# Grams of three chunks moved ahead of the inverses, attention's output product by high and low halves, one weight chunk's place changed

## The chip, the cores and the metric

The kernel runs on one core of a Trainium2 chip. The metric is device time in microseconds (us), the median of three runs; lower is better. TensorE (PE in the profile) does the matrix products, VectorE (DVE) and ScalarE (ACT) the work on elements, GpSimd (POOL) a few small things, and SyncE (SP) issues the weight transfers.

## What is computed

One decoder layer on a sequence of 256 tokens of width 2048, in float32: two token mixers side by side (mLSTM and RWKV-7), merged by gates; cross-attention to 256 memory tokens; a causal convolution with GeGLU. What the change touches is the RWKV-7 scan and the attention's output:

```python
def rwkv7_scan(r, w, k, v, kk, kka):
    def step(state, inp):
        rt, wt, kt, vt, kkt, kat = inp
        state = (state * wt[:, :, None, :]
                 - jnp.einsum('bhvk,bhk->bhv', state, kkt)[..., None] * kat[:, :, None, :]
                 + vt[..., None] * kt[:, :, None, :])
        return state, jnp.einsum('bhvk,bhk->bhv', state, rt)
...
    p = jax.nn.softmax(scores, axis=-1).astype(v.dtype)
    o = jnp.einsum('bhsm,bmhd->bshd', p, v).reshape(B, S, XATTN_WIDTH)
    return o @ wo
```

## The kernel before

**Weights.** Nearly all time goes into products of activations with weights that stream from memory in 648 chunks of 128 x 1024 numbers. A float32 chunk is split: ScalarE casts the high half (wh, L391), VectorE subtracts it for the low half (wl, L421), and TensorE forms three products high x high, low x high, high x low in float32r. In the profile "fm" are such products with 256 columns (the weight held, activations moving) and "tm" those with 512 columns. A chunk's buffer comes free when TensorE has done with the chunk four places earlier, so cast and low half of chunk c+3 are queued when chunk c begins. KICK (L342) lists chunks whose halves are placed some elements further on in their buffer; it changes nothing in the arithmetic.

**Side work.** Everything else is written as Python generators, and the order of all instructions is fixed when the program is written. Twice per chunk (`half()`, called a half step here: six 512-column or twelve 256-column products) the class Spread lets side work run. Each half step adds 640 to VectorE's account and 820 to ScalarE's, up to 1200; a piece of queued work is taken when both accounts are above zero, and what it issues through the metered engines is charged (VectorE 70 + 1.04 per element of a partition, ScalarE 200 + 0.83). Work issued through `nc.vector` and `nc.scalar` isn't charged. A task with a chain runs a piece every so many half steps, whenever neither account is below -700.

**RWKV.** The 256 tokens are cut into 4 chunks of 64; 16 heads are held as 8 pairs (j and e, in two groups hf of four pairs). For each chunk the kernel needs the products of BK (keys) with KR (queries) of all heads, the gram, and the inverse of a unit triangular matrix made from its corner, in 32 x 32 blocks. The task `inverses` (L925) forms the corners alone with 64 small products (gramA), in two bursts; it gathers all 32 x 32 blocks side by side in `comp`, transposes them to A, solves all of them at once on VectorE in 31 steps of a product and a sum (tmp and L), and transposes the result twice into cmt: directly from L, and from Lt, a copy that ScalarE makes with two axes exchanged. When the inverses and the values are there, `start_rwkv` adds the task `rwkv` (L1017), a piece every 3 half steps. Its first piece forms the gram of chunk 0, the next one copies the inverse of chunk 0 to m0 (`diagonal`), the third forms the level-one products (lv) with m0. Then each chunk goes through X, level two, U, the new state (Tn) and the output Y, and while chunk c does that, the gram of chunk c+1 is formed in two halves, one between X and level two and one ahead of U. A gram uses PSUM tiles of the tag aux, of which there are four; sums over heads (bon) use the same tag. U (7) and T2 (6) are tags of larger buffers that all stages share.

**Attention.** The values (xv) come from a tm block whose two halves of columns end one after the other, the probabilities (pT) from four staggered softmax tasks. `xo` (L1719) multiplies them in float32, 8 products, each shown as two records of the profile, and splits the result into oT's halves for the next weight block.

Of the kernel before, what the change touches and what calls it, by code (L numbers as in the profile page):

```python
# [145 lines left out]
def _layer(ctx, tc, nc, d, dbg):  # L146
# [189 lines left out]
    def block(kind, srcs, xs, evac, before=None, cols=512, pool_=None, pre=None, bankwise=False, tail=0):  # L336
# [6 lines left out]
            168: 0, 216: 2, 219: 2, 236: 2, 243: 2, 257: 2, 282: 2}  # L343
# [581 lines left out]
    def inverses():  # L925
# [8 lines left out]
        comp = C("comp", "bg0", [P, 32, 32])  # L934
        for hc in range(4):
            hf, c0 = hc // 2, hc % 2 * 2
            if hc % 2 == 0:
                qs = [aux("gramA", [P, 2, 4, 64]) for _ in range(2)]
                for c in range(4):
                    for j in range(4):  # L940
                        for e in range(2):
                            p = hf * 4 + j
                            mm(qs[c // 2][E2[e], c % 2, j], KR[E2[e], p, c, 0], BK[E2[e], p, c, e])
            q = qs[hc % 2]
            o = comp[:, :, hc * 8:hc * 8 + 8].rearrange("p s u -> p u s")
            v = q.rearrange("p a j s -> p (a j) s")
            dve.tensor_scalar(o, v[:, :, 0:32], ccol("bd", 1), None, op0=ALU.mult)
            dve.scalar_tensor_tensor(o, v[:, :, 32:64], ccol("bd", 1, 32), o, op0=ALU.mult, op1=ALU.add)
            yield
        A = C("A", "au1", [P, 32, 32])  # L950
# [3 lines left out]
        for j in range(31):  # L954

            n = j + 1, 31 - j
# [6 lines left out]
        M["cmt"] = U("cmt", [P, 2, 32, 32])  # L963
        dve.transpose(flat(M["cmt"][:, 0]), flat(L))
        Lt = C("Lt", "au1", [P, 32, 32])
# [51 lines left out]
    def rwkv():  # L1017
# [6 lines left out]
        bg = [C("bg", f"bg{hf}", [P, 2, 512]) for hf in H]  # L1024
        bkt = [bg[hf][:, 0].rearrange("p (j t) -> p j t", j=4) for hf in H]
        gx = [C("gx", f"gx{hf}", [P, 512]) for hf in H]
        gr = [[v.rearrange("p (e j t) -> p e j t", e=2, j=4) for v in (bg[hf][:, 1], gx[hf])] for hf in H]
        au = [C("au", f"au{hf}", [P, 2, 2, 4, 64]) for hf in H]
        ab, uv = [v[:, 0] for v in au], [v[:, 1] for v in au]
# [5 lines left out]
        def gram(c, hf):  # L1035
# [5 lines left out]
            def evac():  # L1041
                for e in H:
                    dve.tensor_mul(ab[hf][:, e], qs[e][:, :, 0:64], bc(sm, 4))
                    dve.tensor_mul(gr[hf][c % 2][:, e], qs[e][:, :, 64:128], bc(im, 4))
            return evac

# [4 lines left out]
        def inverse(c, hf, k):  # L1051
            return cmt[:, k, :, hf * 16 + c * 4:hf * 16 + c * 4 + 4].rearrange("p s j -> p j s")
# [16 lines left out]
        def carried(c):  # L1069
            for hf in H:  # L1070
                for e in H:
                    act.copy(ab[hf][E2[e], e], KR[E2[e], hf * 4:hf * 4 + 4, c, 0])
# [8 lines left out]
        def level1(q, v, more):  # L1081
            for hf, j, e in heads:
                mm(v[quart[1][e], hf, j], ab[hf][quart[0][e], e, j, 32:64], m0[quart[0][e], hf, j])
# [8 lines left out]
        evs = [gram(0, hf) for hf in H]  # L1092
        for ev in evs:
            ev()
        yield
# [4 lines left out]
        level1(*quarter("lv1", 0, (0, 1), True), True)()  # L1100
# [941 lines left out]
```

## Time and profile before

| | |
|---|---|
| median of 3 runs | 1867.37 us (1866.93 to 1867.52) |
| the profiled execution's own time | 1867.02 us |
| its span, first to last instruction | 1865.2 us |
| TensorE busy | 1856.8 us, 15022 products and as many weight loads |
| VectorE busy | 1294.6 us |
| ScalarE busy | 1015.9 us |
| mean granted TensorE clock | 0.999 |

The profile is one execution, taken by the hardware profiler. A product's record covers more than the time until the next one may start, so records overlap: what a product costs TensorE is read from the distance between two starts. Times in a timeline count from the first instruction; merged rows carry xN. "idle before" is time in which an engine had nothing to do, and the name behind it is what it waited for.

### The profile page before, as it was taken

The numbers are of one execution on the slowest core, as the hardware profiler recorded it, in microseconds if no ns is written. First come the engines' busy times: TensorE is split into PE (matmuls) and PEld (weight loads), VectorE is DVE, ScalarE is ACT, GpSimd is POOL, SyncE is SP. The second block draws the span as 40 slices with busy tenths as digits, with TensorE's granted clock in tenths as the row PEclk, the third lists the DMA queues.
The fourth block names the chain that finished last, engine by engine and source line by source line (L and its number), as shares of the span: only waits on it lengthen the run. The fifth ranks groups of instructions, "written<-read, shape, count | busy, mean of one in ns | idle before, by whom it ended". The sixth has DMA issues, their size and how long they took to land.

```text
span 1865.2 us, 36357 instructions
## 1 busy us (share of the span) xinstructions
PE 1856.8 (100%) x15022; PEld 1770.4 (95%) x15022; DVE 1294.6 (69%) x1836; ACT 1015.9 (54%) x1481; POOL 19.9 (1%) x38
## 2 busy tenths in 40 slices
PE   9999999999999999999999999999999999999998
PEld 9999888999999999999999999999999988888887
DVE  7789787666675857687766667776666775556555
ACT  6776445655454646665544445544444554545544
POOL 0000000000000000000000000000000000000000
PEclk9999999999999999999999999999999999999999
DMA  7545544344555765455666666666666666666664
GB/s 264 190 169 195 180 157 159 127 157 159 169 194 196 280 196 180 160 184 173 197 193 196 194 193 195 188 194 197 197 194 194 196 192 214 197 192 192 194 192 145
DMA packets 98197, 351.46 MB, mean 188 GB/s; under 512 B 11056, under 2 KB 11568, under 8 KB 97648
## 3 DMA queue, kind: packets, MB, share of 16 engines
q1 hardware_dynamic: 97168, 348.01, 58.1%
q8 instruction: 117, 1.92, 0.4%
q10 hardware_dynamic: 864, 1.15, 0.2%
q14 instruction: 48, 0.39, 0.1%
HBM read 347.01 MB, written 2.10 MB: 187 GB/s over the span
## 4 chain that ended last, share of the span: by engine, by line
PE 98%; DVE 1%; issue 0%; DMA 0%; ACT 0%; ACTq 0%; DVEq 0%
PE fm L181 68%; PE tm L181 25%; PE gram L181 0%; DVE wl L421 0%; PE Y L181 0%; PE num L181 0%; DMA w<-in_w_in_dram 0%; PE lv L181 0%; DVE ql L66 0%; PE X L181 0%; PE U L181 0%; PE gramA L181 0%; PE zg L181 0%; DVE z L66 0%; PE zwa L181 0%
## 5 line engine op out<-in xcount | busy, mean ns | idle before, releaser
L421 DVE TENSOR_TENSOR wl<-raw,wh 128x1024 fp32r<-128x1024 f32 (+1 forms) x639 | 774.9, 1218 | 412.3 <-ACT wh L391 407.5
L391 ACT CAST wh<-raw 128x1024 fp32r<-128x1024 f32 (+1 forms) x639 | 663.5, 1043 | 481.7 <-PE fm L181 362.3
L181 PE MATMUL fm<-fh,wh 128*128 128x256 f32 x2048 | 564.4, 277 | 0.6 <-DVE fh L66 0.6
L181 PE MATMUL fm<-fh,wl 128*128 128x256 f32 x2048 | 563.4, 276 | 0.0
L181 PE MATMUL fm<-fl,wh 128*128 128x256 f32 x2048 | 563.3, 276 | 0.0
L181 PEld LDWEIGHTS fm<-fh,wh 128*128 128x128 f32 x2048 | 383.6, 188 | 0.8 <-DVE fh L66 0.8
L181 PEld LDWEIGHTS fm<-fl,wh 128*128 128x128 f32 x2048 | 383.5, 188 | 0.0
L181 PEld LDWEIGHTS fm<-fh,wl 128*128 128x128 f32 x2048 | 383.4, 188 | 0.0
L181 PE MATMUL tm<-wh,as 128*128 128x512 f32 x1024 | 315.4, 389 | 0.0
L181 PE MATMUL fm<-hh,wh 128*128 128x256 f32 x1024 | 284.1, 279 | 0.4 <-ACT wh L402 0.3
L181 PE MATMUL fm<-hh,wl 128*128 128x256 f32 x1024 | 281.5, 277 | 0.1
L181 PE MATMUL fm<-hl,wh 128*128 128x256 f32 x1024 | 281.3, 277 | 0.0
L181 PEld LDWEIGHTS tm<-wh,as 128*128 128x128 f32 x1024 | 192.1, 188 | 39.9
L181 PE MATMUL tm<-wl,as 128*128 128x512 f32 x512 | 199.2, 389 | 0.0
L181 PEld LDWEIGHTS fm<-hh,wh 128*128 128x128 f32 x1024 | 191.7, 188 | 2.1 <-ACT wh L402 0.5
L181 PEld LDWEIGHTS fm<-hh,wl 128*128 128x128 f32 x1024 | 191.5, 188 | 0.3 <-DVE wl L421 0.3
L181 PEld LDWEIGHTS fm<-hl,wh 128*128 128x128 f32 x1024 | 191.4, 188 | 0.1
L181 PEld LDWEIGHTS tm<-wl,as 128*128 128x128 f32 x512 | 96.1, 188 | 19.9
L66 ACT CAST as<-ac 128x256 fp32r<-128x256 f32 x128 | 45.6, 404 | 110.8 <-PE tm L181 110.8
L66 DVE TENSOR_TENSOR as<-ac,as 128x256 fp32r<-128x256 f32 x128 | 48.5, 421 | 61.7 <-ACT as L66 61.7
L181 PE MATMUL fm<-mgh,wh 128*128 128x256 f32 x256 | 70.9, 277 | 0.0
L181 PE MATMUL fm<-mgl,wh 128*128 128x256 f32 x256 | 70.8, 276 | 0.0
(386 smaller groups left out, 2214.7 us busy)
## 6 DMA issues: line engine op xcount, KB each, us to landing
raw<-in_w_fu_dram SPq DMA_DIRECT2D x256, 512.0 KB, 4.1
raw<-in_w_in_dram SPq DMA_DIRECT2D x152, 512.0 KB, 3.5
raw<-in_w_fd_dram SPq DMA_DIRECT2D x128, 512.0 KB, 4.0
raw<-in_w_br_dram SPq DMA_DIRECT2D x32, 512.0 KB, 3.8
raw<-in_w_mo_dram SPq DMA_DIRECT2D x32, 512.0 KB, 4.0
raw<-in_w_xk_dram SPq DMA_DIRECT2D x8, 512.0 KB, 3.6
raw<-in_w_xv_dram SPq DMA_DIRECT2D x8, 512.0 KB, 3.5
raw<-in_w_xq_dram SPq DMA_DIRECT2D x8, 512.0 KB, 4.0
```

The costliest lines, as they stand in the source:

```text
L66: return f(out, *a, **k)
L181: pe.matmul(out, lhsT, rhs, start=start, stop=stop, skip_group_check=True)
L391: nc.scalar.copy(wh, r)
L421: nc.vector.tensor_sub(wl, r, self.st[self.nl][0])
```

## The change

The grams of chunks 0, 1 and 2 are formed at the start of `inverses`, in three bursts of three pieces each, and `comp` takes its blocks from them by ScalarE copies; only chunk 3's corners are still made by gramA, with operands exchanged. The products' masked results are kept: chunks 0 and 1 in four T2 tiles, chunk 2 partly in a new U tile (gr2), whose other half is L. The block solve runs on the transposed blocks, so the roles of L and Lt for the two halves of cmt are exchanged. In `rwkv` the first piece is gone, only chunk 3's gram is left in the loop, `early` charges VectorE's account for the others, and the task starts 1 half step after the inverses instead of 4. The attention's probabilities and values are kept as float32r halves, and the output product becomes three float32r products instead of one float32 product. One entry of KICK goes from 282 to 284. Cut to its core:

```diff
-            168: 0, 216: 2, 219: 2, 236: 2, 243: 2, 257: 2, 282: 2}
+            168: 0, 216: 2, 219: 2, 236: 2, 243: 2, 257: 2, 284: 2}
...
-        L = C("L", "au0", [P, 32, 32])
+        sm, im = ccol("sm", 64), ccol("im", 64)
+        comp = C("comp", "bg0", [P, 32, 32])
+        at = comp.rearrange("p t u -> p u t")
...
+        M["ab"] = [[T2("ab", [P, 2, 4, 64]) for _ in range(2)] for _ in range(2)] + [late, late]
+        M["cmt"] = U("cmt", [P, 2, 32, 32])
+
+        def gram(c):
+            ab = M["ab"][c]
+            gr = [M["gr"][hf][c % 2] for hf in range(2)]
+            if c == 2:
+                M["gr2"] = U("gr2", [P, 2, 1024])
...
+            qs = [[aux("gram", [P, 4, 128]) for _ in range(2)] for _ in range(2)]
+            for hf in range(2):
+                for j in range(4):
+                    for e in range(2):
+                        mm(qs[hf][e][:, j], flat(BK[E2[e], hf * 4 + j, c]), flat(KR[E2[e], hf * 4 + j, c]))
+            for hf in range(2):
+                for e in range(2):
+                    nc.vector.tensor_mul(ab[hf][:, e], qs[hf][e][:, :, 0:64], bc(sm, 4))
+                    nc.vector.tensor_mul(gr[hf][:, e], qs[hf][e][:, :, 64:128], bc(im, 4))
+                yield
+            for hf in range(2):
+                for e in range(2):
+                    for b in range(2):
+                        r = slice(e * 64 + b * 32, e * 64 + b * 32 + 32)
+                        nc.scalar.copy(at[r, c * 8 + hf * 4:c * 8 + hf * 4 + 4], ab[hf][r, e, :, b * 32:b * 32 + 32])
+            yield
+
+        def paced(gen):
+            for _ in gen:
+                dve.spent += 672.5
+                yield
+
+        yield from paced(gram(0))
+        yield from paced(gram(1))
+        yield from paced(gram(2))
+        L = M["gr2"][:, 1].rearrange("p (c i) -> p c i", c=32)
         pool.memset(L, 0.0)
...
-        for hc in range(4):
-            hf, c0 = hc // 2, hc % 2 * 2
-            if hc % 2 == 0:
-                qs = [aux("gramA", [P, 2, 4, 64]) for _ in range(2)]
-                for c in range(4):
-                    for j in range(4):
-                        for e in range(2):
-                            p = hf * 4 + j
-                            mm(qs[c // 2][E2[e], c % 2, j], KR[E2[e], p, c, 0], BK[E2[e], p, c, e])
...
+        q = aux("gramA", [P, 8, 64])
+        for p in range(8):
+            for e in range(2):
+                mm(q[E2[e], p], BK[E2[e], p, 3, e], KR[E2[e], p, 3, 0])
...
-            dve.tensor_tensor(o, L[:, 0:j + 1, j].unsqueeze(2).broadcast_to((P,) + n),
-                              A[:, j, j + 1:32].unsqueeze(1).broadcast_to((P,) + n), op=ALU.mult)
-            dve.tensor_add(L[:, 0:j + 1, j + 1:32], L[:, 0:j + 1, j + 1:32], o)
+            dve.tensor_tensor(o, A[:, j + 1:32, j].unsqueeze(2).broadcast_to((P,) + n),
+                              L[:, j, 0:j + 1].unsqueeze(1).broadcast_to((P,) + n), op=ALU.mult)
+            dve.tensor_add(L[:, j + 1:32, 0:j + 1], L[:, j + 1:32, 0:j + 1], o)
...
-        dve.transpose(flat(M["cmt"][:, 0]), flat(L))
+        dve.transpose(flat(M["cmt"][:, 1]), flat(L))
...
-        dve.transpose(flat(M["cmt"][:, 1]), flat(Lt))
+        dve.transpose(flat(M["cmt"][:, 0]), flat(Lt))
...
-            tasks["r"] = side.add(rwkv(), chain=GAP, phase=4)
+            tasks["r"] = side.add(rwkv(), chain=GAP, phase=1)
...
+        def early():
+            dve.spent += 1345.0
...
-        evs = [gram(0, hf) for hf in H]
-        for ev in evs:
-            ev()
-        yield
         diagonal(0)
...
-                ev.append(gram(c + 1, 0))
+                ev.append(gram(c + 1, 0) if c == 2 else early)
...
-                ev.append(gram(c + 1, 1))
+                ev.append(gram(c + 1, 1) if c == 2 else early)
...
+            if c == 0:
+                for hf in H:
+                    nc.scalar.copy(gr[hf][0].rearrange("p e j t -> p (e j t)"), M["gr2"][:, 0, hf * 512:hf * 512 + 512])
...
+            nc.vector.scalar_tensor_tensor(M["xvl"][t][:, c], ps[g][:, t], stm.rc[:, t:t + 1], M["xv"][:, t, c],
+                                           op0=ALU.mult, op1=ALU.subtract)
...
         act.copy(M["pT", h], q)
+        nc.vector.tensor_sub(M["pl"][:, h], q, M["pT", h])
...
-                    mm(q[:, j], M["xv"][:, mt, h * P:(h + 1) * P], M["pT", h][:, mt], start=(mt == 0), stop=(mt == 1))
+                    mm(q[:, j], M["xv"][:, mt, c], M["pT", h][:, mt], start=(mt == 0), stop=False)
+                    mm(q[:, j], M["xv"][:, mt, c], M["pl"][:, h, mt], start=False, stop=False)
+                    mm(q[:, j], M["xvl"][mt][:, c], M["pT", h][:, mt], start=False, stop=(mt == 1))
```

## Rows read from the trace of the kernel before

**Rows 1.** The page, busy times by engine and the chain that ended last

```profile
PE 1856.8 (100%) x15022; PEld 1770.4 (95%) x15022; DVE 1294.6 (69%) x1836; ACT 1015.9 (54%) x1481; POOL 19.9 (1%) x38
...
PE 98%; DVE 1%; issue 0%; DMA 0%; ACT 0%; ACTq 0%; DVEq 0%
```

**Rows 2.** Timeline, TensorE, first gramA burst: start us, us, what, records

```profile
235.00 0.39 PE L181 MATMUL tm<-wh,hl 128*128 128x512 f32 x1
235.23 0.39 PE L181 MATMUL tm<-wl,hh 128*128 128x512 f32 x1
235.55 2.08 PE L181 MATMUL gramA<-BK,KR 64*64 64x64 f32 x64
237.56 0.50 PE L181 MATMUL tm<-wh,hh 128*128 128x512 f32 x1
237.90 0.39 PE L181 MATMUL tm<-wh,hl 128*128 128x512 f32 x1
```

**Rows 3.** Timeline, TensorE, the gram of chunk 0

```profile
289.50 2.06 PE L181 MATMUL gram<-KR,BK 64*128 64x128 f32 x32
291.48 0.50 PE L181 MATMUL tm<-wh,hh 128*128 128x512 f32 x1
```

**Rows 4.** Timeline, TensorE, half of the gram of chunk 1

```profile
306.34 1.16 PE L181 MATMUL gram<-KR,BK 64*128 64x128 f32 x16
307.44 0.69 PE L181 MATMUL lv<-mt,m 32*32 32x32 f32 x32
```

**Rows 5.** Timeline, VectorE, the inverses and what follows

```profile
248.08 1.24 DVE L66 STREAM_TRANSPOSE A<-comp 128x1024 f32<-128x1024 f32 x1
...
286.08 1.25 DVE L66 STREAM_TRANSPOSE cmt<-L 128x1024 f32<-128x1024 f32 x1
288.30 1.25 DVE L66 STREAM_TRANSPOSE cmt<-Lt 128x1024 f32<-128x1024 f32 x1 [0.97 <-ACT Lt L66]
...
291.71 0.42 DVE L66 TENSOR_TENSOR au<-gram,con 128x256 f32<-128x256 f32 x1
...
294.36 2.35 DVE L421 TENSOR_TENSOR wl<-raw,wh 128x1024 fp32r<-128x1024 f32 x2
296.63 0.49 DVE L66 COPY m<-cmt 128x128 f32<-128x128 f32 x2
```

**Rows 6.** Timeline, ScalarE, the same stretch

```profile
286.14 2.13 ACT L66 COPY Lt<-L 128x1024 f32<-128x1024 f32 x1 [1.83 <-DVE L L66]
288.17 2.95 ACT L391 CAST wh<-raw 128x1024 fp32r<-128x1024 f32 x3
294.35 1.05 ACT L391 CAST wh<-raw 128x1024 fp32r<-128x1024 f32 x1 [3.24 <-PE tm L181]
295.43 1.70 ACT L66 COPY au<-vt 64x256 f32<-64x256 f32 x4
```

**Rows 7.** Timeline, TensorE, the level-one products of chunk 0

```profile
300.09 0.69 PE L181 MATMUL lv<-m,au 32*32 32x32 f32 x32
```

**Rows 8.** Timeline, three engines, attention's output product

```profile
777.27 1.23 DVE L421 TENSOR_TENSOR wl<-raw,wh 128x1024 fp32r<-128x1024 f32 x1 [2.56 <-ACT wh L391]
...
778.67 3.62 PE L181 MATMUL xo<-pT,xv 128*128 128x256 f32 x16
...
779.35 0.85 ACT L66 ACTIVATE xv<-tm,stm_c 128x256 f32<-128x256 f32 x2
...
781.94 0.59 PE L181 MATMUL fm<-oT,wh 128*128 128x256 f32 x2
...
782.36 0.28 PE L181 MATMUL fm<-oT,wl 128*128 128x256 f32 x1
```

**Rows 9.** Windows, fm products alone: window, us, busy (count) by engine, clock, DMA

```profile
864.00:872.00 8.00, 8.00 (x70) 8.00 (x69) 0.57 (x1) 0.00 (x0) 1.00 0.45 136
941.00:1381.00 440.00, 440.00 (x3885) 440.00 (x3884) 28.04 (x41) 0.00 (x0) 1.00 0.63 194
```

**Rows 10.** Windows, the end: PE, PEld, DVE, ACT, POOL busy (count), clock, DMA

```profile
1858.00:1865.00 7.00, 1.63 (x7) 0.78 (x5) 2.68 (x4) 2.00 (x7) 0.00 (x0) 0.84 0.59 219
```

More of the change, by code (lines that the diff above doesn't have):

```diff
@@ L930, in inverses @@
         flat = lambda v: v.rearrange("p a b -> p (a b)")
-        L = C("L", "au0", [P, 32, 32])
+        sm, im = ccol("sm", 64), ccol("im", 64)
+        comp = C("comp", "bg0", [P, 32, 32])
+        at = comp.rearrange("p t u -> p u t")
+        odd = C("bg", "bg1", [P, 2, 512])
+        gx = [C("gx", f"gx{hf}", [P, 512]) for hf in range(2)]
+        M["gr"] = [[v.rearrange("p (e j t) -> p e j t", e=2, j=4) for v in (gx[hf], odd[:, hf])] for hf in range(2)]
+        M["au"] = [C("au", f"au{hf}", [P, 2, 2, 4, 64]) for hf in range(2)]
@@ new lines, in inverses @@
+        late = [v[:, 0] for v in M["au"]]
+        M["ab"] = [[T2("ab", [P, 2, 4, 64]) for _ in range(2)] for _ in range(2)] + [late, late]
[5 more added lines that the diff above has]
+                M["gr2"] = U("gr2", [P, 2, 1024])
+                gr = [M["gr2"][:, 0, hf * 512:hf * 512 + 512].rearrange("p (e j t) -> p e j t", e=2, j=4) for hf in range(2)]
+            qs = [[aux("gram", [P, 4, 128]) for _ in range(2)] for _ in range(2)]
[14 more added lines that the diff above has]
+            yield
@@ L950, in inverses @@
-        A = C("A", "au1", [P, 32, 32])
+        q = aux("gramA", [P, 8, 64])
+        for p in range(8):
+            for e in range(2):
+                mm(q[E2[e], p], BK[E2[e], p, 3, e], KR[E2[e], p, 3, 0])
+        o = at[:, 24:32]
+        nc.vector.tensor_scalar(o, q[:, :, 0:32], ccol("bd", 1), None, op0=ALU.mult)
+        nc.vector.scalar_tensor_tensor(o, q[:, :, 32:64], ccol("bd", 1, 32), o, op0=ALU.mult, op1=ALU.add)
+        dve.spent += 672.5
+        yield
+        A = M["cmt"][:, 0]
@@ L1023, in rwkv @@
         heads = [(hf, j, e) for hf in H for j in range(4) for e in H]
[L1024 to L1029, printed above, removed]
+        bg = C("bg", "bg0", [P, 2, 512])
+        bkt = [bg[:, hf].rearrange("p (j t) -> p j t", j=4) for hf in H]
+        gr = M["gr"]
+        ab, uv = M["ab"], [v[:, 1] for v in M["au"]]
         m0, m1 = [C("m", f"m{i}", [P, 2, 4, 32]) for i in H]
@@ L1051, in inverse @@
         def inverse(c, hf, k):
-            return cmt[:, k, :, hf * 16 + c * 4:hf * 16 + c * 4 + 4].rearrange("p s j -> p j s")
+            return cmt[:, k, :, c * 8 + hf * 4:c * 8 + hf * 4 + 4].rearrange("p s j -> p j s")
         def diagonal(c):
@@ L1071, in carried @@
                 for e in H:
-                    act.copy(ab[hf][E2[e], e], KR[E2[e], hf * 4:hf * 4 + 4, c, 0])
+                    act.copy(ab[c][hf][E2[e], e], KR[E2[e], hf * 4:hf * 4 + 4, c, 0])
                     act.copy(uv[hf][E2[e], e], T[hf][E2[e]])
@@ L1079, in quarter, with level1 @@
             return q, q[:, 0:256].rearrange("p (h j s) -> p h j s", h=2, j=4)
-        def level1(q, v, more):
+        def level1(c, q, v, more):
             for hf, j, e in heads:
-                mm(v[quart[1][e], hf, j], ab[hf][quart[0][e], e, j, 32:64], m0[quart[0][e], hf, j])
+                mm(v[quart[1][e], hf, j], ab[c][hf][quart[0][e], e, j, 32:64], m0[quart[0][e], hf, j])
             def evac():
@@ L1164, in rwkv @@
                     mm(qy[E2[e], hf, j], KR[E2[e], hf * 4 + j, c, 1], T[hf][E2[e], j], start=False)
-            f = level1(*lv1, c + 1 < 3) if more else None
+            f = level1(c + 1, *lv1, c + 1 < 3) if more else None
             if more:
@@ L1656, in vx_half @@
         if g == 0:
-            M["xv"] = C("xv", "bg0", [P, 2, 512])
+            M["xv"] = C("xv", "bg0", [P, 2, 512], F32R)
+            M["xvl"] = [C("xvl", f"gx{t}", [P, 512], F32R) for t in range(2)]
+        c = slice(g * S, (g + 1) * S)
         for t in range(2):
-            act.activation(M["xv"][:, t, g * S:(g + 1) * S], ps[g][:, t], AF.Copy, scale=stm.rc[:, t:t + 1])
+            act.activation(M["xv"][:, t, c], ps[g][:, t], AF.Copy, scale=stm.rc[:, t:t + 1])
+            nc.vector.scalar_tensor_tensor(M["xvl"][t][:, c], ps[g][:, t], stm.rc[:, t:t + 1], M["xv"][:, t, c],
+                                           op0=ALU.mult, op1=ALU.subtract)
     def vx_evac(ps):
```

22 lines of the change are left out of this document (8 added, 14 removed).

## The prediction

> **What bounds the kernel now.** I read the page first: its busy times and its chain of waits. TensorE is busy for the whole span, VectorE for 69% and ScalarE for 54% of it, and the chain that ended last lies on TensorE for 98% [rows 1]. So the time is the sum of the distances between the starts of TensorE's instructions: an instruction taken off it is gained in full, a burst of other work costs its entry and exit as well, and work on VectorE or ScalarE costs nothing until TensorE has to wait for it. The timeline of TensorE gives the price of each burst [rows 2 to 4], that of VectorE and ScalarE the only long chain that the change pushes towards TensorE [rows 5, 6], which ends at the first level-one product of the RWKV chain [rows 7]. Then I read the attention's output product [rows 8] and the pace of the 256-column products [rows 9].
>
> **Grams on TensorE.** An ordinary 512-column product starts every 0.23 us. The first gramA burst (64 records, 32 products) lies between the products at 235.23 and 237.90, 2.67 us with two ordinary steps in it, so it costs 2.21; its body is 237.56 - 235.55 = 2.01, entry and exit together 0.20 [rows 2]. There are two such bursts: 4.42 us go. The big gram of chunk 0 (32 records) has a body of 291.48 - 289.50 = 1.98, and with the same entry and exit costs 2.18 [rows 3]; it goes from its old place. In the chain the grams of chunks 1 and 2 stand between other fp32 products, whose entry and exit stay: each half costs 307.44 - 306.34 = 1.10 [rows 4], and four halves go, 4.40 us (the other three measure 1.09). Added ahead of the inverses: three bursts of 32 records, each like the one of chunk 0, 3 x 2.18 = 6.54; and gramA for chunk 3 alone, half a burst, 1.00 + 0.20 = 1.20. If nothing waited, that is 6.54 + 1.20 - 4.42 - 2.18 - 4.40 = -3.26 us.
>
> **When the inverses are ready.** Here I think most of that is lost. The side work runs one piece per half step of six products (6 x 0.227 = 1.36 us). A new gram piece puts 672.5 on VectorE's account, as each of the four old gramA pieces did, and 640 come back per half step, so ten pieces in place of four make the inverses end six half steps later. The RWKV task starts one half step after them instead of four, and its own first piece (the gram, then a gap of three) is gone: its copies of the inverse stay at the same half step, but the last transpose of the inverses is now one half step ahead of them and not seven. Before, VectorE ended that transpose at 289.55 and made the copies at 296.63 to 297.12 [rows 5], 3 us ahead of the level-one products at 300.09 [rows 7].
>
> Now the new chain. The transpose into A started at 248.08 [rows 5]. It moves by six half steps (8.2) and by what TensorE does more ahead of it (6.54 + 1.20 - 4.42 = 3.3), and by up to 1.3 more, because the second gram needs four PSUM banks and one of them holds head sums whose evacuation stands on VectorE behind a weight half, which stands behind the cast on ScalarE, which now stands behind eight small copies; I take 0.8. That gives 260.4. From there to the transpose of L took 286.08 - 248.08 = 38.0 us [rows 5], VectorE without a gap; one half step fewer lies in between now, so half a weight half (1.17 for one, from the two in 2.35) less: 37.4, to 297.8. Then, in order: ScalarE's copy Lt, 2.13 [rows 6], to 300.0; queued behind it on ScalarE the cast of weight chunk 102 (2.95 for three, so 0.98), to 301.0; VectorE's half of that chunk, 1.17, to 302.2, which stands ahead of the last transpose on VectorE; that transpose, 1.2, to 303.4; another weight half to 304.6; the copies, 0.49, to 305.1 [rows 5]. TensorE, with 6.54 + 1.20 - 4.42 - 2.18 = 1.14 more work, would reach the level-one products at 301.2, or 302.0 after the bank's wait. So it stands still for some 3 us, and the products start at 305.1 instead of 300.09: **+5.0**. The bank's wait is inside this and isn't counted again. Bounds: 3.9 if the bank's wait doesn't come (A starts 0.8 earlier, and a little is won behind it), 6.1 if ScalarE's copies are dear.
>
> The eight copies per gram (32 partitions, 128 elements each, written 32 elements apart) aren't in the trace. The cast of 1024 takes 1.05 and a copy of 256 takes 1.70 / 4 = 0.43 [rows 6], and a line through the two gives 0.32 for 128; the copy Lt, which reads 32 elements apart, takes 2.13 for 1024, 1.1 more, or 0.14 per 128. So 0.32 to 0.46; I take the low end, since the new copies read in order, and below 0.40 they end before VectorE is free for A and change little; at 0.46 the third set ends late and the chain is 1.1 longer. The Trainium skill (page "SBUF — State Buffer", section "Door 1: The DMA port swizzle") says that an access which goes to a new 16-byte line each time pays a penalty; by that the dear end would hold, and the sum would be 1 us more.
>
> After the level-one products the four removed halves give 4.40 back. The eight evacuations of a chunk's gram are moved, not added (they took 294.36 - 291.71 = 2.65 [rows 5]); VectorE's whole work up to the copies grows only from 4 x 1.4 + 2.65 = 8.2 to 3 x 2.65 + 1.4 = 9.3, the 1.4 being an estimate for a pair of gramA's evacuations. The two later copies of chunk 2's gram, some 0.6 us each on ScalarE, lie in a gap of three half steps (4.1 us); if that gap were full they would delay one level-one copy by 1.2. The memsets of L move to a POOL that is busy for 1% of the span. No DMA is moved. The seven U and six T2 buffers are full with the new tiles but hold them.
>
> **Attention.** 16 records from 778.67 to 781.94, 3.27 us [rows 8], become 24 single products; at 113.3 ns (440 us / 3883 products [rows 9]) 2.72, so -0.55, and the slow first product behind the fp32 burst (781.94 to 782.36 for two and a bit) should go, -0.2. Against it: the low halves of V are made on VectorE after the weight half at 777.27, and the second pair after ScalarE's activations at 779.35 to 780.20 [rows 8] and the low half of the last head: two of some 0.45 each, to about 781.1. The last products must wait for that, and start the block at about 782.0, as before. So I count only the softer exit and the pace behind it, **-0.25**, between -0.8 and +0.6. The Trainium skill (page "FP8 and Floating Point Precision", section "TensorE Precision Notes") gives a true fp32 product four passes; 32 passes against 24 would be -0.8, with nothing waiting.
>
> **The moved chunk.** Between 864 and 872 the fm products start every 8000 / 68 = 117.6 ns, elsewhere every 113.3 (the two begun before the window taken off) [rows 9]. Chunk 284 lies in that slow stretch, 282 ahead of the burst that begins it again. If a chunk at another place ends such a stretch, two chunks of 24 products gain 4.3 ns each: **-0.2**; the other end is 0.
>
> **Sum:** 5.0 - 4.40 - 0.25 - 0.2 = +0.15, against the profiled execution's own 1867.02 (a span of 1865.2 and 1.8 around it): 1867.2. That execution lies 0.35 below the median of the runs. With the bounds of the chain (3.9 to 6.1), of attention, and half a microsecond for slow stretches of other lengths, this case gives 1865.3 to 1869.2.
>
> **Rivals.** *The inverses are ready in time.* Then the whole -3.26 shows, with -0.45: 1863.3, up to 1864.1 with the bank's wait. For it: 3 us of slack before, and only 1.1 us more work on VectorE. Against: the order of the queues above, one half step instead of seven.
>
> *The clock falls behind the wait.* In the last 7 us of the span TensorE is busy for 1.63 us and the mean granted clock is 0.84 [rows 10]: it fell to the lower level (1.2 GHz) for some 2.2 us, after TensorE had stood still for nearly 3. A standstill of 3 us or more ahead of the level-one products could do the same; at half pace for 2 to 8 us it adds 1 to 4 us, 1868.2 to 1871.2. The Trainium skill has a rule for it (page "TensorE: Matmul & The Clock Gate", section "Why this matters for your kernels"): idle gaps in mid-kernel bring the clock down to half. No row of mid-kernel here shows such a gap; the end of the span agrees, with 0.84.
>
> *The FFN keeps the slow pace (slower than before).* The pace of fm products depends on how the stream starts again after a burst. Nothing interrupts it from 941 on: 3883 products in 440 us [rows 9]. If the last burst of transposes before 941 leaves the slow pace, they cost 4.3 ns more each, 17 us: 1884. It decides there and nowhere else. Against: no work of that stage changes.
>
> **How the numbers follow.** Chances: my forecast 0.64, ready in time 0.23, clock 0.09, slow pace 0.04. A measurement of this kernel can tell about 0.2% (3.7 us) from no change, so faster means below 1863.6: half of the second case and the lower tail of the first. Faster 0.19, same 0.70, slower 0.11. The range takes in the second case whole and the nearer half of the clock's: 1863.1 to 1869.8.
>
> **What would show it.** Right: a wait of TensorE for VectorE's copy m<-cmt of 2 to 4 us just before 305, the level-one products at 304 to 306, four distances X to lv and bkt to U without a gram, xo as 24 products with small waits for VectorE, 113 ns from about 866. Wrong: no wait for m, so that the level-one products start by 302.5; a granted clock below 1 there; or 118 ns behind 941.

## The result: 3.8 us slower, and the profile after

The changed kernel took 1870.78 us (median of 9 runs, 1868.97 to 1873.68), the kernel before 1866.93 (9 runs, 1866.63 to 1867.95): a ratio of 1.0019, 95% interval 1.0010 to 1.0027. That is slower by 0.2%, just at what a measurement of this kernel can tell, and 1 us above the upper end of the predicted range. The runs also spread over 4.7 us where those before spread over 1.3. The profiled execution took 1871.49, with a span of 1869.7.

Where the time went is read by laying the two traces side by side: TensorE's order of work is the same in both but for the grams and the output product, so the start of the first product of each weight chunk (counted from 0 in the order of use) can be compared. The differences of the two profiled executions:

| first product of weight chunk | before, us | after, us | after - before | step |
|---|---|---|---|---|
| 81, behind the first burst of grams | 237.56 | 237.83 | +0.27 | +0.27 (start of the kernel) |
| 100, behind the other bursts | 294.34 | 295.89 | +1.55 | +1.28 |
| 102, behind the level-one products | 300.71 | 305.58 | +4.87 | +3.32 |
| 103 | 303.59 | 310.72 | +7.13 | +2.26 |
| 118, behind the four removed halves | 368.90 | 372.70 | +3.80 | -3.33 |
| 258, behind the attention | 787.77 | 792.56 | +4.79 | +0.99 |
| 647, the last | 1854.75 | 1859.30 | +4.55 | -0.24 |

The page after, busy times and the chain that ended last (they answer to [rows 1]):

```profile
PE 1857.4 (99%) x14934; PEld 1770.0 (95%) x14934; DVE 1295.2 (69%) x1838; ACT 1026.6 (55%) x1507; POOL 19.9 (1%) x38
...
PE 96%; DVE 2%; ACT 1%; issue 1%; DMA 0%; SPq 0%; DVEq 0%; ACTq 0%
```

Eighty-eight TensorE records fewer, as the change says, and yet 0.6 us more of busy time: some of the products that remain took longer. VectorE and ScalarE now hold 3% of the chain that ended last. The waits of TensorE name two of the places:

```profile
PE lv L181 <- DVE m L66: 2.9, 1, 2.9
...
PE X L181 <- ACT au L66: 0.4, 1, 0.4
```

The timeline of VectorE around the inverses (it answers to [rows 5]):

```profile
260.44 1.24 DVE L66 STREAM_TRANSPOSE cmt<-comp 128x1024 f32<-128x1024 f32 x1
...
297.70 1.25 DVE L66 STREAM_TRANSPOSE cmt<-gr 128x1024 f32<-128x1024 f32 x1
300.86 1.23 DVE L421 TENSOR_TENSOR wl<-raw,wh 128x1024 fp32r<-128x1024 f32 x1 [1.92 <-ACT wh L391]
302.01 1.24 DVE L66 STREAM_TRANSPOSE cmt<-Lt 128x1024 f32<-128x1024 f32 x1
303.17 1.18 DVE L421 TENSOR_TENSOR wl<-raw,wh 128x1024 fp32r<-128x1024 f32 x1
304.27 0.45 DVE L66 COPY m<-cmt 128x128 f32<-128x128 f32 x2
```

The same stretch of ScalarE (to [rows 6]), with the first set of the new copies ahead of it:

```profile
237.50 1.73 ACT L962 COPY comp<-ab 32x128 f32<-32x128 f32 x4 [0.72 <-DVE ab L955]
...
297.75 2.13 ACT L66 COPY Lt<-gr 128x1024 f32<-128x1024 f32 x1 [6.27 <-DVE gr L66]
299.77 2.01 ACT L391 CAST wh<-raw 128x1024 fp32r<-128x1024 f32 x2
```

And TensorE at the first of the new grams (to [rows 2, 3]), at the level-one products (to [rows 7]), and at X of chunk 1:

```profile
235.85 2.06 PE L181 MATMUL gram<-KR,BK 64*128 64x128 f32 x32
237.83 0.50 PE L181 MATMUL tm<-wh,hh 128*128 128x512 f32 x1
...
301.34 0.38 PE L1084 MATMUL lv<-con,BK 128*128 128x128 f32 x2
304.59 1.06 PE L181 MATMUL lv<-m,ab 32*32 32x32 f32 x32 [2.88 <-DVE m L66]
305.58 0.80 PE L181 MATMUL tm<-wh,hh 128*128 128x512 f32 x1
...
359.06 0.68 PE L181 MATMUL X<-au,ab 128*64 128x64 f32 x14 [0.40 <-ACT au L66]
```

The late inverses came as worked out: the transpose into A at 260.44 (forecast 260.4), that of L at 297.70 (297.8), the last transpose at 302.01 (302.2), the copies at 304.27 (304.6), the level-one products at 304.59 (305.1). Then something follows that the sum did not hold. TensorE's windows (us; busy time and count of PE, PEld, DVE, ACT, POOL; granted clock; DMA share; GB/s):

```profile
301.00:303.00 2.00, 0.71 (x5) 0.34 (x3) 2.00 (x2) 1.93 (x4) 0.00 (x0) 1.00 0.00 0
303.00:305.00 2.00, 0.41 (x16) 0.41 (x18) 2.00 (x5) 1.41 (x3) 0.00 (x0) 0.68 0.75 260
305.00:307.00 2.00, 2.00 (x29) 1.68 (x24) 1.97 (x4) 0.36 (x1) 0.00 (x0) 0.50 0.72 252
307.00:309.00 2.00, 2.00 (x6) 1.58 (x5) 0.62 (x2) 1.32 (x2) 0.00 (x0) 0.50 0.57 209
309.00:311.00 2.00, 2.00 (x7) 1.52 (x7) 0.91 (x1) 0.28 (x1) 0.00 (x0) 0.62 0.24 84
311.00:313.00 2.00, 2.00 (x28) 1.57 (x28) 1.19 (x1) 0.77 (x1) 0.00 (x0) 1.00 0.69 244
```

The granted clock is 1.00 up to 303, falls while TensorE stands still, is 0.50 (1.2 GHz of 2.4) from 305 to 309, and is back before 311. In that stretch the products of 512 columns start every 0.427 us instead of 0.227, and the level-one products ahead of them take 0.99 us instead of 0.63. This is the second rival of the prediction. The Trainium skill says so too (page "TensorE: Matmul & The Clock Gate", section "Why this matters for your kernels": gaps between bursts in mid-kernel bring the clock back down to half), and here the trace agrees, with 0.50 behind a wait of 2.88 us.

The attention's stretch, timeline of the three engines (to [rows 8]), first VectorE:

```profile
781.21 1.23 DVE L421 TENSOR_TENSOR wl<-raw,wh 128x1024 fp32r<-128x1024 f32 x1 [0.26 <-ACT wh L391]
782.36 0.48 DVE L1697 SCALAR_TENSOR_TENSOR xvl<-tm,stm_c,xv 128x256 fp32r<-128x256 f32 x1
783.37 0.48 DVE L1697 SCALAR_TENSOR_TENSOR xvl<-tm,stm_c,xv 128x256 fp32r<-128x256 f32 x1 [0.54 <-ACT xv L66]
...
785.47 0.48 DVE L1697 SCALAR_TENSOR_TENSOR xvl<-tm,stm_c,xv 128x256 fp32r<-128x256 f32 x1 [0.54 <-ACT xv L66]
```

ScalarE:

```profile
781.07 0.48 ACT L66 ACTIVATE xv<-tm,stm_c 128x256 fp32r<-128x256 f32 x1
782.87 0.47 ACT L66 ACTIVATE xv<-tm,stm_c 128x256 fp32r<-128x256 f32 x1 [1.31 <-DVE xvl L1697]
```

TensorE:

```profile
782.62 0.36 PE L181 MATMUL xo<-pT,xv 128*128 128x256 f32 x1
...
786.94 0.40 PE L181 MATMUL fm<-oT,wh 128*128 128x256 f32 x2
```

The output product takes 786.94 - 782.62 = 4.32 us; before, it was 3.27 [rows 8]. The second scaling on ScalarE waits for the first subtraction on VectorE, and the next subtraction for that scaling: the two engines take turns, and TensorE waits in between.

### The profile page after: what moved, and what is told of

Read it like the earlier page. It is cut to its first block, busy times and chain, and to the rows that moved or that the text cites. A ratio compares the mean times of both kernels' runs of the same rounds, so it can differ in the third digit from the quotient of the medians.

```text
span 1869.7 us, 36215 instructions
## 1 busy us (share of the span) xinstructions
PE 1857.4 (99%) x14934; PEld 1770.0 (95%) x14934; DVE 1295.2 (69%) x1838; ACT 1026.6 (55%) x1507; POOL 19.9 (1%) x38
## 4 chain that ended last, share of the span: by engine, by line
PE 96%; DVE 2%; ACT 1%; issue 1%; DMA 0%; SPq 0%; DVEq 0%; ACTq 0%
PE fm L181 67%; PE tm L181 25%; DVE wl L421 1%; PE gram L181 0%; PE Y L181 0%; DMA w<-in_w_in_dram 0%; PE num L181 0%; ACT wh L391 0%; PE lv L181 0%; DVE ql L66 0%; PE U L181 0%; PE X L181 0%; PE zg L181 0%; DVE z L66 0%; PE zwa L181 0%
```

## The experiments

The theory after these traces: the standstill of 2.9 us and the clock behind it cost more than the removed grams give back, and the attention adds 1 us. The rivals: the loss lies in the attention, or in VectorE as a whole, so that a mend in one place moves the wait to another. The kernel before was run beside each; its medians were 1867.2 to 1867.5. This table has the differences to the profiled execution of before at the same places as above, for every trace that follows. The start of an execution varies by up to 1.8 us (column 81; TensorE waits 0.2 to 2.4 us for the first casts), so the steps between columns are what counts.

| profiled execution | 81 | 100 | 102 | 103 | 118 | 176 | 216 | 258 | 647 |
|---|---|---|---|---|---|---|---|---|---|
| changed | +0.27 | +1.55 | +4.87 | +7.13 | +3.80 | +3.79 | +3.79 | +4.79 | +4.55 |
| changed, again | +1.56 | +2.84 | +5.78 | +7.34 | +3.76 | +3.75 | +3.75 | +4.76 | +4.52 |
| wait filled | +0.26 | +1.54 | +4.59 | +4.57 | +0.97 | +0.96 | +5.03 | +5.93 | +5.67 |
| wait filled, again | +0.70 | +1.98 | +5.03 | +5.00 | +1.41 | +2.33 | +6.65 | +9.46 | +9.20 |
| wait filled, 178 moved | 0.00 | +1.27 | +4.33 | +4.30 | +0.71 | +1.25 | +5.47 | +6.41 | +6.16 |
| RWKV later | +0.47 | +1.75 | +0.81 | +1.17 | -2.09 | +6.06 | +10.12 | +11.03 | +10.81 |
| transpose first | +1.47 | +2.75 | +2.75 | +2.90 | -0.70 | -0.71 | -0.71 | +0.13 | -0.13 |
| attention as before | -0.02 | +1.26 | +4.18 | +5.76 | +2.18 | +2.17 | +2.17 | +2.40 | +2.15 |
| scalings first | +0.12 | +1.40 | +4.31 | +5.88 | +2.29 | +2.29 | +2.29 | +2.19 | +1.93 |
| both mends | +0.25 | +1.54 | +1.54 | +1.68 | -1.93 | -1.94 | -1.94 | -1.76 | -2.00 |
| both, 178 moved | +0.56 | +1.84 | +1.84 | +1.99 | -1.61 | -1.61 | -1.44 | -1.51 | -1.77 |
| both, 257 not moved | -0.18 | +1.10 | +1.10 | +1.24 | -2.36 | -2.36 | -2.36 | -2.60 | -2.86 |
| and copies shared | +1.61 | +2.89 | +2.89 | +3.00 | -1.35 | -1.35 | -1.36 | -1.61 | -1.87 |

### Products in the wait

```
+            if c == 0:
+                for _ in range(7):
+                    mm(q[:, 0:256], ones.broadcast_to((P, P)), ones.broadcast_to((P, 256)))
             for hf, j, e in heads:
                 mm(v[quart[1][e], hf, j], ab[c][hf][...], m0[...])
```

> Seven fp32 products of 128x256 on constants, 0.41 us each by the old xo, stand on TensorE directly ahead of the first level-one products and write a part of their bank that these overwrite; 2.9 us of work where TensorE stood still. Theory (the standstill itself brings the clock down): granted clock 1.00 behind them, the products at 227 ns from the first, the level-one products at the same time as in the changed kernel give or take 0.2, 2.3 us below its profiled execution, 1869.2, and a scatter of about 1.3 us in place of 4.7. Rival (the clock falls in that place for another reason, or in chance executions): products at 427 ns again and 1870.8 or more.

Measured: 1870.09 (1868.18 to 1874.75, 11 runs), ratio 1.0015 (1.0007 to 1.0024). TensorE's timeline in this kernel, and then its windows:

```profile
301.54 3.21 PE L181 MATMUL lv<-ones 128*128 128x256 f32 x14
304.68 0.69 PE L181 MATMUL lv<-m,ab 32*32 32x32 f32 x32
305.31 0.50 PE L181 MATMUL tm<-wh,hh 128*128 128x512 f32 x1
```

```profile
303.00:305.00 2.00, 2.00 (x29) 1.50 (x29) 2.00 (x5) 1.37 (x3) 0.00 (x0) 1.00 0.79 260
305.00:307.00 2.00, 2.00 (x31) 1.69 (x26) 1.97 (x4) 0.37 (x1) 0.00 (x0) 1.00 0.79 248
```

The level-one products start where they did (304.68 against 304.59), the clock stays 1.00, and the step from chunk 102 to 103 is -0.02 instead of +2.26. So the fall of the clock belongs to the standstill, and this half of the expectation is shown. The other half fell: the runs spread over 6.6 us with no fall of the clock (over the 29 executions of this and the two like kernels below, the mean granted clock is 0.999 or 1.000, as in the kernel before; over the 20 of the changed kernel it is 0.997 to 0.999), and the profiled run lost 4.07 us between chunks 176 and 216, where the changed kernel loses nothing. That is taken up below.

### The changed kernel again

No edit.

> The changed kernel once more, for a second trace. Theory (the wait is fixed by the chain of VectorE and ScalarE, the time at the lower clock behind it is not): the same wait of 2.8 to 2.9 us at the level-one products, a lower clock behind it that lasts longer or shorter than in the first trace, 0 to 4 us of loss, and 1869 to 1873.7 for the runs. Rival (the lower clock behind the wait always costs the same): 2.3 us of loss again, and the spread is something else.

Measured: 1871.59 (1870.24 to 1873.77, 11 runs), ratio 1.0023 (1.0014 to 1.0032). The wait is 2.9 us again, and the step behind it (102 to 103) is +1.56 this time. A window of it:

```profile
307.00:309.00 2.00, 2.00 (x6) 1.61 (x5) 1.61 (x3) 0.33 (x2) 0.00 (x0) 0.50 0.57 227
```

In the two kernels with other attention code the step is +1.58 and +1.57. So the wait is fixed to about 0.1 us, and the price of the clock behind it was 1.6 us in three traces and 2.3 in one, within the 1 to 4 that the rival was given. The traces show what differs: in the first one the clock fell 0.9 us ahead of the level-one products and stood at 0.50 for 6.8 us, in the other three it fell 0.8 to 1.6 us behind their start and stood there for 3.4 us. In the first one the level-one products lost another 0.36 us to it, which the step to chunk 102 holds.

### The RWKV task three half steps later

```
-            tasks["r"] = side.add(rwkv(), chain=GAP, phase=1)
+            tasks["r"] = side.add(rwkv(), chain=GAP, phase=4)
```

> Only the phase of the RWKV task changes, 1 to 4 half steps, so that its copies of the inverse come 4.1 us later in TensorE's order. Theory (TensorE stands still because the products come too early in its order, and the clock falls because it stood still): no wait for m<-cmt, granted clock 1.00 throughout the stretch, 3.3 + 2.3 = 5.6 us below the profiled execution of the changed kernel, 1865.9, give or take 0.7 for slow stretches that begin elsewhere; the scatter of the runs as small as that of the kernel before. Rival (the chain of VectorE and ScalarE is late whatever TensorE does, so the wait comes back a little later in the RWKV chain): a new wait of 1 us or more at another product, 1868 or more.

Measured: 1878.09 (1870.44 to 1880.27, 6 runs), ratio 1.0044 (1.0027 to 1.0061). Up to chunk 118 the theory holds: no wait for m, clock 1.00 in every window from 301 to 313, and the trace stands 2.09 us ahead of the kernel before where the changed kernel is 3.80 behind it. Then the rival holds, with a longer way round than it said. TensorE's waits in this kernel:

```profile
PE zg L181 <- ACT gwh L66: 1.5, 1, 1.5
...
PE zg L181 <- DVE gwl L66: 0.8, 1, 0.8
...
PE zg L181 <- DVE gwh L66: 0.4, 1, 0.4
```

ScalarE's timeline just ahead of them:

```profile
520.29 0.62 ACT L66 CAST gwh<-gup 128x512 fp32r<-128x512 f32 x1 [2.96 <-DMA gup<-in_g_up_dram]
```

The gate's weights `gup` are loaded into the buffers `au0` and `au1`, which come free when the RWKV chain ends. A later chain means a later load (issued 12.0 us behind the start of chunk 160 instead of 5.7), ScalarE stands 2.96 us for it, and TensorE 2.7 for the gate. The chain had no three half steps to give. Behind these waits the clock falls too, though the longest of them is 1.5 us, with one or two products between each and the next:

```profile
532.90:536.20 3.30, 3.15 (x15) 3.18 (x16) 1.02 (x3) 0.62 (x1) 0.00 (x0) 0.50 0.37 146
```

And from chunk 162 on the products keep a slow pace (more of it below). The trace is that of a run of 1877.74; two of the six runs took 1870.4 and 1870.8, and no trace shows what they were spared.

### The last transpose first

```
         act.copy(Lt, L.rearrange("p c i -> p i c"))
-        yield
         dve.transpose(flat(M["cmt"][:, 0]), flat(Lt))
+        M["m"] = [C("m", f"m{i}", [P, 2, 4, 32]) for i in range(2)]
+        for hf in range(2):
+            dve.tensor_copy(M["m"][0][:, hf], M["cmt"][:, 0, :, hf * 4:hf * 4 + 4].rearrange("p s j -> p j s"))
...
-            tasks["r"] = side.add(rwkv(), chain=GAP, phase=1)
+            tasks["r"] = side.add(rwkv(), chain=GAP, phase=2)
...
-        diagonal(0)
         transposed(0)
```

> The last transpose of the inverses follows ScalarE's copy of L at once on VectorE, ahead of the low halves of two weight chunks, and the copy of chunk 0's inverse stands directly behind it; the RWKV task starts so that its products keep their places in TensorE's order. Theory (the wait is made by the two weight halves, which nobody needs yet, and by a cast queued behind the copy of L; the chain itself would be ready at 301.6): the wait for m<-cmt falls from 2.9 us to under 0.5, the granted clock stays 1.00, nothing of the RWKV chain ends later, 2.6 + 2.3 = 4.9 us below the profiled execution of the changed kernel and a little more by the slow pace behind it: 1865.6 to 1866.6. Rival (VectorE is full, so whatever is moved ahead makes something else late): TensorE waits as long for the weight half of chunk 102 or 103, and the time stays above 1869.

Measured: 1866.19 (1865.34 to 1867.51, 11 runs), ratio 0.9992 (0.9983 to 1.0001). No wait for m is left, the clock is 1.00, and the RWKV chain keeps its place: +2.75 at chunk 102 as at chunk 100. The wait had been made by the order of two queues. The timeline of VectorE there, taken from the run with both mends (below), and of TensorE:

```profile
297.68 1.25 DVE L66 STREAM_TRANSPOSE cmt<-gr 128x1024 f32<-128x1024 f32 x1
299.91 1.25 DVE L66 STREAM_TRANSPOSE cmt<-Lt 128x1024 f32<-128x1024 f32 x1 [0.98 <-ACT Lt L66]
301.19 0.50 DVE L66 COPY m<-cmt 128x128 f32<-128x128 f32 x2
301.61 2.35 DVE L421 TENSOR_TENSOR wl<-raw,wh 128x1024 fp32r<-128x1024 f32 x2
...
301.63 0.69 PE L181 MATMUL lv<-m,ab 32*32 32x32 f32 x32
302.25 0.50 PE L181 MATMUL tm<-wh,hh 128*128 128x512 f32 x1
```

The copies stand at 301.19 instead of 304.27, in time for TensorE at 301.63. What the rival feared, the weight half of chunk 102, comes behind them and just in time: it costs the +0.14 between chunks 102 and 103.

### The attention: as before, or both scalings first

The first run takes the attention's code of the kernel before into the changed kernel; the second changes only the order:

```
         for t in range(2):
             act.activation(M["xv"][:, t, c], ps[g][:, t], AF.Copy, scale=stm.rc[:, t:t + 1])
+        for t in range(2):
             nc.vector.scalar_tensor_tensor(M["xvl"][t][:, c], ps[g][:, t], stm.rc[:, t:t + 1], M["xv"][:, t, c], ...)
```

> The attention's output product, its operands and their copies are those of the kernel before; grams, inverses and the moved chunk are those of the changed kernel. Theory (the late inverses carry the loss: a wait of 2.9 us at the level-one products and 2.3 us of halved clock behind it, and attention adds 0.9 us): about 0.9 us below the changed kernel, 1869.9 against 1870.8, with the wait for m<-cmt and a granted clock below 1 behind it still there. Rival (the loss lies mainly in the attention, whose waits and slow pace run on behind it): 3 us or more below, about 1867.

> Only the order in the half of V changes: both scalings on ScalarE are written ahead of both subtractions on VectorE. Theory (the second scaling waits for the first subtraction because both touch one tile, so the two engines take turns and the last subtraction ends at 785.95): the scalings follow each other as before, 0.85 us for two, the two waits of TensorE within xo of 0.28 and 0.24 us and most of the two small ones go, 0.5 to 0.8 us below the changed kernel, 1870.0 to 1870.3. Rival (the subtractions are late anyway because they stand behind the weight half on VectorE): less than 0.2 us below, 1870.6 to 1870.8.

Measured: 1869.22 (1867.38 to 1872.46), ratio 1.0010 (1.0001 to 1.0019), and 1869.39 (1868.66 to 1871.14), ratio 1.0009 (1.0000 to 1.0017), 11 runs each. The wait for m is there in both (2.9 and 2.8 us), with a clock below 1 behind it. From chunk 118 to 258 the steps are +0.22 and -0.10, against +0.99 in the changed kernel. So the attention's share is 0.8 us, and all of it the taking of turns: with both subtractions behind both scalings it is gone, with the same work on every engine. The product itself then takes 3.50 us, against 4.32 in the changed kernel and 3.27 in the kernel before: 24 products at 113 ns would be 2.72, so by itself the new product gains nothing here. The medians fell by 1.4 to 1.6, more than that; the clock cost 0.7 less in both traces, and the runs spread.

### Both mends, and one chunk moved back

> The mends of the two runs together: the last transpose first, and both scalings ahead of both subtractions. Theory (the two losses are independent): the gains add, 0.9 us below the run with the transpose alone, 1864.7 to 1865.7, 1 to 2 us under the kernel before. Rival (what is won ahead of the attention is lost there or behind it): the same as the run with the transpose alone, 0.3 us or less below it.

Measured: 1865.31 (1864.53 to 1865.88, 11 runs), ratio 0.9988 (0.9979 to 0.9997). The gains add, as expected, and the runs spread over 1.4 us.

Behind the new output product the stream of fm products starts at 113 ns a product, and chunk 257, at the other place, runs at 120 within it; before, the stream started slow and the same chunk ended that. So in the next run its entry is taken out of `KICK`:

```
-            168: 0, 216: 2, 219: 2, 236: 2, 243: 2, 257: 2, 284: 2}
+            168: 0, 216: 2, 219: 2, 236: 2, 243: 2, 284: 2}
```

> Both mends, without the other place of weight chunk 257. Theory (with the new output product its stream starts fast, and a chunk at another place in a fast stream costs 24 products 6.7 ns each): 0.2 us below the run with both mends, 1865.1 against 1865.3. Rival (the stream would turn slow without it and stay so to the next burst at chunk 264, six chunks): 0.5 us above it.

Measured: 1864.98 (1864.12 to 1867.50, 11 runs), ratio 0.9990 (0.9982 to 0.9999). In its trace chunk 257 runs at 113 ns and so does what follows (from 256 to 258 the step is -0.39, with both mends alone -0.23). The times cannot carry 0.2 us: five of the eleven runs lie at 1866.5 and above, the other six at 1865.0 and below. The trace carries it; what sets those five runs apart is not shown.

### Copies on two engines

X of chunk 1 stood 0.40 us for ScalarE (the last line of TensorE's timeline after the change, above). Of ScalarE's eight copies per chunk (for three chunks) the four from T go to VectorE, which is idle there:

```
-                    act.copy(uv[hf][E2[e], e], T[hf][E2[e]])
+                    nc.vector.tensor_copy(uv[hf][E2[e], e], T[hf][E2[e]])
+                    act.spent += 412.48
```

> Both mends, no other place for chunk 257, and of the sixteen copies that carry the state into a later chunk (eight for each of two chunks that the X products read, and eight for the last) the half from T on VectorE instead of ScalarE. Theory (the fourth removed half of a gram was eaten by X of chunk 1, which stands 0.40 us for ScalarE's last copy, with 0.57 us at that step in all): the copies end 1.5 us earlier, X's wait goes, the products X to lv cost what they cost in chunk 0, 0.5 us below the run without them on two engines, the median about 0.5 us further under the kernel before than its 2.4 us, 1864.5. Rival (VectorE's copies stand behind its own weight halves and come later than ScalarE's did): X waits for VectorE, 0.4 us or more, and no gain.

Measured: 1863.75 (1863.32 to 1865.93, 11 runs), ratio 0.9982 (0.9973 to 0.9991), before 1867.23. The timeline of VectorE, ScalarE and TensorE there:

```profile
351.06 1.24 DVE L1110 COPY au<-T 64x256 f32<-64x256 f32 x4
...
351.72 1.67 ACT L66 COPY ab<-KR 64x256 f32<-64x256 f32 x4
...
353.38 1.15 PE L181 MATMUL X<-au,ab 128*64 128x64 f32 x32
354.46 0.69 PE L181 MATMUL lv<-mt,m 32*32 32x32 f32 x32
```

X runs through, 354.46 - 353.38 = 1.08 us without a wait. From chunk 114 to 115 the difference falls by 1.07, a whole half of a gram, where it fell by 0.26 in the changed kernel. This version beats both kernels, the one before by 0.18%.

### What spreads the runs

> Both mends, and weight chunk 178 staged at the other place of kind 2. Theory (the scatter of the runs is a fm stream that falls from 113.3 to 117.8 ns where a weight half arrives just in time at chunk 176, and keeps that pace to the next burst at chunk 215, 38 chunks or 4.1 us): a chunk at another place ends it two chunks later; the highest times come down by up to 4 us, the lowest rise by 0.2 us (24 products at 120 ns), and the spread of the runs falls under 2.5 us where it is 4 to 6 without it. Rival (the scatter comes from elsewhere, the clock or the transfers): the spread is that of the run without it, and all times are 0.2 us higher.

The edit is one more entry, `178: 2`, in `KICK`. Measured with both mends: 1865.21 (1864.77 to 1866.41, 11 runs), ratio 0.9989 (0.9980 to 0.9998). There was no spread to take away, so this run settles nothing but the price: 0.17 us (176 to 216). The same entry then went into the kernel that did spread, beside that kernel once more:

> The seven products in the wait, and weight chunk 178 staged at the other place of kind 2. Theory (the spread of the kernel with the seven products, 1868.2 to 1874.8 though its clock never fell, is the slow pace that begins at chunk 176 when a transfer ahead of it lands late): with the pace ended at 178 the highest run stays under 1871, the lowest is 0.2 us higher than without, the median comes down to about 1869. Rival (the spread comes from other places): highest run above 1872, as without it.

> The seven products in the wait once more, on the same chip as the run with chunk 178 moved, for a second trace. Theory (chance decides at chunk 176): a spread of 4 us or more again, and in the trace either the slow pace from 176 to 215 with the weight half of 176 less than 0.3 us ahead, or the fast pace with 0.5 us. Rival (this kernel takes the slow pace always): the slow pace from 176 to 215 with the half in time.

Measured: 1869.84 (1868.62 to 1874.42, 11 runs), ratio 1.0017 (1.0008 to 1.0025), and 1873.23 (1869.39 to 1876.14, 7 runs), ratio 1.0030 (1.0019 to 1.0040). The mend failed: the highest run is still above 1874, and in the trace the slow pace runs over chunk 178 to the burst at 215. But the cause is seen in all three traces of this kernel. Windows of fm products alone, in the first of them (us; busy time and count of PE, PEld, DVE, ACT; clock; DMA):

```profile
540.00:552.00 12.00, 12.00 (x108) 12.00 (x107) 2.05 (x3) 0.00 (x0) 1.00 0.52 169
560.00:660.00 100.00, 100.00 (x852) 100.00 (x851) 6.85 (x10) 2.67 (x6) 1.00 0.69 233
```

The same view of the changed kernel, the second of these stretches:

```profile
563.00:659.00 96.00, 96.00 (x849) 96.00 (x848) 6.83 (x10) 2.67 (x6) 1.00 0.69 238
```

With the two begun before the window taken off, that is 100 us / 850 = 117.6 ns a product against 96 / 847 = 113.3, at a clock of 1.00 in both. And ScalarE's timeline ahead of it, in the run with chunk 178 moved:

```profile
515.75 0.62 ACT L66 CAST gwh<-gup 128x512 fp32r<-128x512 f32 x1 [0.34 <-DMA gup<-in_g_up_dram]
517.45 1.26 ACT L66 CAST gwh<-gup 32x512 fp32r<-32x512 f32 x2 [1.08 <-DMA gup<-in_g_up_dram]
```

In the three slow traces a load of the gate's weights landed late: the second of the four took 4.77, 5.46 and 5.84 us from issue to landing, and ScalarE waited for them 0.64, 1.42 and 1.79 us in all (TensorE, for the gate, up to 0.71). In the ten others whose RWKV chain keeps its place the second load took 3.85 to 4.18, and ScalarE waited at most 0.38. Everything on ScalarE and VectorE behind it shifts, and the tightest weight half of that stage, that of chunk 176, ends 0.15, 0.05 and 0.05 us ahead of the chunk's third product, the first that needs it, instead of 0.51. With that product and the next, the stream falls behind by 0.01 us in the first of these traces and by 0.18 in the two others, and from there on it keeps 117.6 ns, up to chunk 216 in two traces and up to 236 in the third. So a hold of 0.2 us or less costs 4 us and more. That the hold itself turns the pace is argued from these three traces against the ten; no run changes the hold alone. What stays open is why the load came late in three of three traces of the kernel with the wait filled and in none of the changed kernel, and so how much of the changed kernel's own spread is this, and how much the clock.

## Why the prediction was wrong

It said +0.15 on the profiled execution, and it became +4.55. Of the 4.40 missed, the clock is 2.26, the attention 1.24 and the removed halves 1.07; the start of the execution adds 0.27, and the inverses take 0.40 off. By its own steps:

- **Grams on TensorE.** Right. The part ahead of the level-one products was to cost 1.14 and cost 1.28, from chunk 81 to 100. The first burst's body, 237.83 - 235.85 = 1.98, is that of [rows 3]. The wait for a PSUM bank that was put at 0.8 did not come; VectorE waited 1.69 us for gramA instead, and that A stood at 260.44 all the same is luck.
- **When the inverses are ready.** Right, to 0.8 us and within the bounds given: +5.0 was forecast for the level-one products, and they began 304.59 - 300.09 = 4.50 later, 4.23 without the later start of the execution; to chunk 102 it was 4.87 - 0.27 = +4.60, in which they already ran at the lower clock. The reason given, one half step and two queues in place of seven half steps, is shown by the run that turns the queue round: no wait is left, and nothing else becomes late. The eight copies took 1.73 / 4 = 0.43 us each, near the dear end of 0.32 to 0.46. That is the side on which the prediction's page of the Trainium skill ("SBUF — State Buffer", section "Door 1: The DMA port swizzle") put them, though they were not what delayed A.
- **The clock.** This is the first step that failed. The sum took a standstill of 3 us as the price of a standstill of 3 us, and gave the clock's fall behind it a chance of 0.09, with "no row of mid-kernel here shows such a gap". The one row that did show such a gap, at the end of the span [rows 10], had the mean clock at 0.84, and should have made this the likeliest case; the standstill there was also read too long, since the clock fell at 1862.8, 2.3 us behind the last product's end. It cost 1.6 to 2.3 us behind chunk 102, and the run with the wait filled shows that it comes from the standstill. The rival's range, 1868.2 to 1871.2, holds the median.
- **The four removed halves.** -4.40 was forecast, and -3.33 came (-3.58 in the second trace). At three of the four places 1.05 to 1.11 came, at X of chunk 1 only 0.26: it had had no slack, and when TensorE came earlier, ScalarE's copies were late by 0.40 us, with a slower X and a slow stretch of products besides. With the copies on two engines -4.35 comes (3.00 to -1.35). The step that failed is that a removed half is gained in full wherever TensorE is busy.
- **Attention.** -0.25 was forecast, and +0.99 came. The prediction put VectorE's subtractions behind ScalarE's, but saw no wait of ScalarE for VectorE, and had the last of them end at 781.1. With the 3.8 us by which all this now comes later that is 784.9; it ended at 785.47 + 0.48 = 785.95. With both scalings first the step is -0.10 in that run and +0.17 with both mends. Only with chunk 257 left at its place as well, which the prediction did not think of, is it -0.24 to -0.26, and this comes behind the product and not in it.
- **The moved chunk.** -0.2 was forecast. From chunk 258 to the end it was -0.24. Chunk 284 itself ran at 120.1 ns a product, and the slow pace ended behind it.
- **The range.** It ended at 1869.8 because the clock's case was given so little. The spread of 4.7 us between runs was not thought of at all: two things here end in chance, how long the clock stays down (6.8 us in one trace, 3.4 in three) and, in the kernel with the wait filled, a load that lands late.

So the terms were right wherever nothing waited. The version with all the mends has them all: +1.39 to chunk 103 (1.14), -4.35 (-4.40), -0.26 (-0.25), -0.26 (-0.2), in sum -3.48, close to the first rival, "ready in time", with its -3.26 - 0.45. The change is sound; what it lost, it lost where TensorE came to wait for the order of work on VectorE and ScalarE.

## What to carry to other kernels

When a chain on slower engines is pushed towards the engine that bounds the kernel, look at what is queued between its last steps: here two weight halves that nobody needed yet, and a cast behind a copy, made 2.9 us of wait out of none. Price a forecast standstill of TensorE with the clock behind it, from the nearest row that shows one, and look at the slack of each later wait before a removed instruction is counted as a gain. Where one engine rounds a tile and another subtracts from it part by part, write all the roundings first.

## What the runs showed of the hardware that was not expected

- Behind a wait of 2.8 to 2.9 us the granted clock fell to half in each of the four traces that have one, and products worth 1.6 to 2.3 us of loss ran before it was back. In the run with the later RWKV chain it fell behind three waits of 1.48, 0.84 and 0.42 us, one or two products apart. With 3.21 us of products on constants in its place it stayed 1.00 (three traces).
- A stream of 256-column products has two paces at a granted clock of 1.00, 113.3 and 117.6 ns, and in three traces the slow one began where two products were held back by 0.01 to 0.18 us in all, and lasted 110 us or more. A chunk at another place ended the slow pace at 284, where the change put it, and not at 178.
- A load of 64 KB, issued at the same place of the order, landed after 3.85 to 4.18 us in ten executions and after 4.77 to 5.84 in three.
